# A hybrid attention and SSD layer in float32: attention in rounds of two units, first tables on another queue, softplus and one product moved

## The chip, the cores and the metric

One Trainium2 chip, one core. The metric is the device time of one execution in microseconds (us), as the median of several runs.

## What is computed

One decoder layer over 2048 positions of width 1024, batch 1, all in float32. A projection of the input gives q, k, v and a gate for 16 attention heads of 64, and the inputs of a Mamba-2 mixer with its gate and its step sizes. Attention is causal and runs three times, with dilations 1, 4 and 16, over a window of 128 steps; the three results are combined by a softmax over their log-sums. Both branches are gated and normed, projected together and normed with the residual.

```python
def dilated_window_attention(q, k, v, slopes, dilation):
    qb = to_blocks(q); kk = with_prev(to_blocks(k)); vv = with_prev(to_blocks(v))
    scores = jnp.einsum('bnqrhe,bnkrhe->bnrhqk', qb, kk)
    ...
    scores = jnp.where(valid, scores - slopes * dist, -jnp.inf)
    lse = jax.nn.logsumexp(scores, axis=-1)
    o = jnp.einsum('bnrhqk,bnkrhe->bnqrhe', jnp.exp(scores - lse[..., None]), vv)
...
wts = jax.nn.softmax(jnp.stack([l1, l2, l3], axis=0), axis=0)
y_att = wts[0] * o1 + wts[1] * o2 + wts[2] * o3
y_att = rms_norm(y_att * jax.nn.silu(z_att), att_norm_g)
dt = jax.nn.softplus(dt_raw + dt_bias)
y_ssm = rms_norm((ssd_chunked(xs, dt, -jnp.exp(a_log), b, c) + d_skip * xs) * jax.nn.silu(z_ssm), ssm_norm_g)
x = layer_norm(alpha * x + jnp.concatenate([y_att, y_ssm], -1) @ w_out, ln_g, ln_b)
```

## The kernel before

The program runs through three stages. In the **projections** (to 1197 us) the products of 2x2 blocks are formed by seven products of sums and differences; each operand is split into a high and a low part, and three matmuls (L340, L342, L344) make up one full product. `products` does seven such steps of twelve matmuls, with a `flush()` after each. `flush` counts and calls whatever was put down for that count in the table `later`: evacuations, weight loads, convolution taps, and the pieces of the generator `decays`. That generator computes the softplus of the step sizes on DVE (a polynomial: L496 and L497 once for each coefficient), then `adt`, a cumulative sum by matmul with a triangle (L510), and its transposes. Before, one piece is called at each count from 14 on, and every coefficient is a piece.

In **attention** (1198 to 1682 us) a unit is four blocks: two heads by two blocks of 128 queries. There are 8 pairs of heads, three dilations (d = 0, 1, 2), four groups `qd` and two halves: 192 units. A unit's scores (L894) go into two PSUM banks. DVE adds the table of biases and takes the minimum in one instruction (L900), ScalarE (ACT) takes the exponentials (L906), PE transposes them (L921), DVE copies the transposes to SBUF (L923), and PE multiplies by v (L947). A block whose keys reach into the block before has 192 columns of scores and not 128; the 64 remaining ones are transposed apart (L929) into a bank of the transposes, copied (L932) and multiplied by v too. That is so for all blocks but those at the start of a sequence, so d = 0 has none, and seven of the eight other groups of a pair have them. After both halves the accumulators N0 and N1, one bank each, are copied to SBUF by ACT (L971, L974, L977). `permute` on POOL reorders q and k for a dilation beforehand. The work of earlier pairs (softmax weights, combination, norm) is called at given units by the tables behind `todo`.

In the **output stage** (to the end) the SSM half is multiplied first, then the attention half (`product`, L1130 to L1132). POOL and DVE make high and low parts (L1098) and combine the last pair (L1038, L1042, L1053); the transposed statistics go through memory (L999, and back by a gather, L1005).

PE, DVE, ACT and POOL run their instructions in the order in which the code calls them; the order of the SyncE queue is set by the scheduler. The loop over the units, before:

```python
for i in range(len(todo) + TA + 1):
    if i < len(todo):
        pts[i] = scores(pairs[pr], d, qd, half)
    if 0 <= i - TA < len(todo):
        pts[i - TA] = transposes(d, qd, half, pts[i - TA])
    if i > TA:
        values(pairs[pr], d, qd, half, pts.pop(i - TA - 1))
```

Of the kernel before, what the change touches and what calls it, by code (L numbers as in the profile page):

```python
# [16 lines left out]
S = 2048  # L17
# [11 lines left out]
def hybrid_layer(ctx, tc, xT, xc, w52, wv, convw, convb, dtb, alog, dskp, gcol, wout,  # L29
# [53 lines left out]
    with ExitStack() as c1:  # L83
# [385 lines left out]
        def decays(dp):  # L469
# [249 lines left out]
        with tc.manual_schedule(engines={E.PE, E.DVE, E.Activation, E.Pool}):  # L719
# [9 lines left out]
            for j in range(16):  # L729
                later.setdefault(14 + j, []).append(lambda: next(dps, None))  # L730
# [66 lines left out]
    with ExitStack() as c2:  # L797
# [22 lines left out]
        def load_tab(A, d):  # L820
# [4 lines left out]
            nc.sync.dma_start(tb, tabs[2 * pr:2 * pr + 2, :, c0:c0 + tb.shape[2]].rearrange("h p c -> p h c"))  # L825
# [56 lines left out]
        def scores(A, d, qd, half):  # L882

            P = io.tile([128, 2, 512], F32, name="P", bufs=3)
            tab = A["tab"][d]
            sp = [psS.tile([128, 512], F32, name="S") for h in range(2)]
            for i in range(2):
                blk, cs = 4 * qd + 2 * i + half, cols(d, qd, half, i)
                for h in range(2):
                    for a in range(2):  # L890
                        o, kv = sp[h][64 * a:64 * a + 64, cs], keys(A, d, qd, 2 * i + half, h, a)
                        if d:
                            o = o.rearrange("p (c r j) -> p c r j", r=kv.shape[2], j=4)
                        nc.tensor.matmul(o, A["q"][d][64 * h:64 * h + 64, blk, 64 * a:64 * a + 64], kv,  # L894
                                         start=True, stop=True)
            for h in range(2):
                for i in range(2):
                    blk, cs = 4 * qd + 2 * i + half, cols(d, qd, half, i)
                    t = tab[:, h, 0:128] if cs.stop - cs.start == 128 else tab[:, h, 128:320]
                    nc.vector.tensor_tensor_reduce(P[:, h, cs], sp[h][:, cs], t, -0.125, 3.0e38, OP.add, OP.min,  # L900
                                                   accum_out=stat(A, 0, d, h, blk))
            for h in range(2):
                for i in range(2):
                    blk, cs = 4 * qd + 2 * i + half, cols(d, qd, half, i)
                    p = P[:, h, cs]
# [10 lines left out]

        def transposes(d, qd, half, P):
            tp = psT.tile([128, 2, 2, 128], F32, name="T")
            for h in range(2):
                for i in range(2):  # L920
                    nc.tensor.transpose(tp[:, h, i], P[:, h, 256 * i:256 * i + 128], ident)  # L921
            pt = io.tile([128, 2, 2, 128], F32, name="PT", bufs=4)
            nc.vector.tensor_copy(pt, tp)  # L923
            new = [i for i in range(2) if not first(d, qd, 2 * i + half)]
            if not new:
                return pt, None
            tc_ = psT.tile([128, 2, 2, 128], F32, name="T")
            for h in range(2):
                nc.tensor.transpose(tc_[:, 0, h], P[:, h, 128:256], ident)  # L929
            pc = io.tile([128, 2, 128], F32, name="PC", bufs=2)  # L930
            rows = slice(64 * new[0], 128)
            nc.vector.tensor_copy(pc[rows], tc_[rows, 0])  # L932
            return pt, pc

        def values(A, d, qd, half, pts):

            pt, pc = pts
            if half == 0:
                if qd == 0:
                    A["num"].append(cm_.tile([128, NR, NJ], F32, name="num", bufs=6))  # L940
# [3 lines left out]
            out = lambda i, h, lo, hi: A["N"][i][64 * h:64 * h + 64, 128 * half + lo:128 * half + hi]  # L944

            def mm(o, l, r, start):
                nc.tensor.matmul(o, l, r, start=start, stop=True, skip_group_check=True)  # L947
            for i in range(2):
                m = at(2 * i + half)
                if first(d, qd, 2 * i + half):  # L950
                    for h in range(2):
                        mm(out(i, h, 0, 128), v[:, m, 64 * h:64 * h + 64], pt[:, h, i], half == 0)
                    continue
                for a in range(2):
                    for h in range(2):
                        w = (v, vs)[a != i][:, m - (a == i == 0 or a != i), 64 * h:64 * h + 64]
                        mm(out(i, h, 64 * a, 64 * a + 64), w, pt[:, h, i, 64 * a:64 * a + 64], half == 0 and a == 0)
            for a in range(2):
                for i in range(2):
                    m, rows = at(2 * i + half), slice(64 * i, 64 * i + 64)  # L960
                    if first(d, qd, 2 * i + half):
                        continue
                    for h in range(2):
                        w = v[rows, m - i] if a == i else vs[rows, m - 2 * i]
                        mm(out(i, h, 64 * a, 64 * a + 64), w[:, 64 * h:64 * h + 64],
                           pc[rows, h, 64 * a:64 * a + 64], False)
            if half == 1:
                for i in range(2):
                    nm = A["N"][i][:, 0:256]
                    if d == 0:  # L970
                        nc.scalar.copy(f2(num[:, 4 * qd + 2 * i:4 * qd + 2 * i + 2, :]), nm)  # L971
                    elif d == 1:
                        o = num.rearrange("p (b s) (n a j) -> p n b a s j", b=4, a=2, j=16)[:, qd, 2 * i:2 * i + 2]
                        nc.scalar.copy(o, nm.rearrange("p (b a s j) -> p b a s j", b=2, a=2, s=4))  # L974
                    else:
                        j = 8 * (4 * qd + 2 * i)
                        nc.scalar.copy(num[:, :, j:j + 16].rearrange("p r (n j) -> p n r j", j=4),  # L977
                                       nm.rearrange("p (n r j) -> p n r j", r=16, j=4))
# [93 lines left out]

        def row():
            return f2(io.tile([128, 2, 512], F32, name="P", bufs=3))
# [43 lines left out]
        pns = ["N0", "N1"]  # L1118

        def product(n, br, hf):  # L1120
# [15 lines left out]
            pns.append(pns.pop(0))  # L1136
            pn = psN.tile([128, 512], F32, name=pns[0])
# [255 lines left out]
```

## Time and profile before

| what | before |
|---|---|
| median of 3 runs | 2076.76 us (2074.23 to 2078.97) |
| profiled execution | 2075.44 us |
| its span, first to last instruction | 2073.7 us |
| mean granted clock of TensorE | 0.980 |
| PE busy | 1979.9 us (95%) |
| DVE busy | 1234.0 us (60%) |
| ACT busy | 1121.9 us (54%) |
| POOL busy | 1077.9 us (52%) |

Busy time counts the instructions of an engine that does work, not its register and branch instructions. PE is TensorE's matmuls, PEld its loads of weights, which run beside them. The granted clock is a share of 2.4 GHz; the lower level is 1.2 GHz. A row in order of time gives start, duration, engine, line and operation, output and inputs, shapes, how many instructions of that kind follow each other; in brackets the idle time of the engine before it and what ended it. "issue" is time in which the engine waited for nothing that the profile shows.

### The profile page before, as it was taken

The numbers are of one execution on the slowest core, as the hardware profiler recorded it, in microseconds if no ns is written. First come the engines' busy times: TensorE is split into PE (matmuls) and PEld (weight loads), VectorE is DVE, ScalarE is ACT, GpSimd is POOL, SyncE is SP. The second block draws the span as 40 slices with busy tenths as digits, with TensorE's granted clock in tenths as the row PEclk, the third lists the DMA queues.
The fourth block names the chain that finished last, engine by engine and source line by source line (L and its number), as shares of the span: only waits on it lengthen the run. The fifth ranks groups of instructions, "written<-read, shape, count | busy, mean of one in ns | idle before, by whom it ended". The sixth has DMA issues, their size and how long they took to land.

```text
span 2073.7 us, 42402 instructions
## 1 busy us (share of the span) xinstructions
PE 1979.9 (95%) x15744; PEld 1616.6 (78%) x15744; DVE 1234.0 (60%) x3166; ACT 1121.9 (54%) x3095; POOL 1077.9 (52%) x963
## 2 busy tenths in 40 slices
PE   8999989889999999979999999999998979999998
PEld 8999778778887888858888867676766767888886
DVE  2353566357877656634444358777777846565553
ACT  3433445346655666536566478887887852232221
POOL 4545346556655666745555322787666572422222
PEclk9999999999999999989999999999999989999999
DMA  9897888967678877896877655788877799232220
GB/s 306 273 306 236 289 305 296 342 226 222 204 218 301 277 258 248 321 367 229 280 244 254 229 219 142 225 233 240 239 221 221 227 275 319 91 118 98 89 69 31
DMA packets 238846, 481.51 MB, mean 232 GB/s; under 512 B 38448, under 2 KB 111664, under 8 KB 226480
## 3 DMA queue, kind: packets, MB, share of 16 engines
q1 hardware_dynamic: 148464, 200.30, 30.8%
q0 software_dynamic: 44816, 180.71, 25.7%
q10 hardware_dynamic: 45360, 97.80, 14.5%
q8 instruction: 124, 2.03, 0.4%
q14 instruction: 82, 0.67, 0.1%
HBM read 323.15 MB, written 163.97 MB: 235 GB/s over the span
## 4 chain that ended last, share of the span: by engine, by line
PE 79%; DMA 7%; ACT 4%; DVE 4%; issue 3%; POOL 2%; SPq 1%; ACTq 0%; POOLq 0%; DVEq 0%
PE pp L340 12%; PE pp L342 11%; PE pp L344 11%; PE N L947 6%; PE pp L151 6%; PE S L894 4%; PE S L1130 4%; PE S L1132 4%; PE S L1131 4%; PE T L921 4%; PE ss L151 3%; ACT P L906 3%; PE T L1130 2%; PE T L1131 2%; PE T L1132 2%
## 5 line engine op out<-in xcount | busy, mean ns | idle before, releaser
L296 POOL TENSOR_TENSOR w<-wr,w 128x512 fp32r<-128x512 f32 x231 | 307.5, 1342 | 223.6 <-ACT w L295 174.5
L906 ACT ACTIVATE P<-P,st 128x192 f32<-128x192 f32 (+1 forms) x768 | 322.0, 421 | 77.3 <-DVE st L900 72.6
L900 DVE CUSTOM_DVE_ANT_0 P<-S,tb 128x192 f32<-128x192 f32 (+1 forms) x768 | 206.6, 324 | 101.3 <-PE S L894 75.7
L349 ACT COPY ev<-pp 128x512 f32<-128x512 f32 x176 | 103.1, 586 | 252.6 <-PE pp L344 227.5
L357 DVE TENSOR_TENSOR ev<-pp,ev 128x512 f32<-128x512 f32 x152 | 101.0, 685 | 149.7 <-PE pp L344 104.1
L295 ACT CAST w<-wr 128x512 fp32r<-128x512 f32 x231 | 139.7, 619 | 43.0 <-DVE wr L288 26.8
L1038 POOL TENSOR_TENSOR wb<-num,wb 128x2048 f32<-128x2048 f32 x21 | 95.7, 4556 | 117.6 <-DMA wb<-d_wd 63.9
L906 ACT ACTIVATION_READ_ACCUMULATOR P<-P,st 128x1 f32 x768 | 144.4, 188 | 0.0
L288 DVE TENSOR_TENSOR wr<-wr 128x512 f32<-128x512 f32 x132 | 123.3, 934 | 25.7 <-DMA wr<-w 21.1
L947 PE MATMUL N<-PT,v 128*64 128x64 f32 (+1 forms) x1536 | 127.1, 263 | 10.1 <-ACT num L971 7.7
L923 DVE COPY PT<-T 128x512 f32<-128x512 f32 x192 | 131.7, 686 | 6.1 <-PE T L921 6.1
L921 PE MATMUL T<-ident,P 128*128 128x128 f32 x768 | 128.8, 291 | 0.4 <-ACT num L977 0.2
L921 PEld LDWEIGHTS T<-ident,P 128*128 128x128 f32 x768 | 82.4, 143 | 48.4 <-issue 24.1
L894 PE MATMUL S<-k,ex 64*64 64x192 f32 (+1 forms) x2048 | 113.1, 332 | 4.7 <-issue 4.7
L947 PEld LDWEIGHTS N<-PT,v 128*64 128x64 f32 x1536 | 79.5, 139 | 48.0 <-issue 20.0
L441 DVE SCALAR_TENSOR_TENSOR ss<-U,cw,ss 128x512 f32<-128x512 f32 x144 | 105.9, 751 | 6.8 <-ACT ss L437 4.5
L122 POOL TENSOR_TENSOR vl<-vraw,vh 128x346 fp32r<-128x346 f32 (+1 forms) x48 | 48.5, 1011 | 91.6 <-ACT vh L121 88.3
L1168 POOL TENSOR_TENSOR k<-k,wb 128x1024 f32<-128x1024 f32 x8 | 25.8, 3227 | 121.9 <-DVE k L1167 121.9
L1106 DVE TENSOR_REDUCE tb<-P 128x128 f32<-128x1024 f32 x30 | 60.0, 2001 | 44.9 <-ACT P L1103 22.5
L894 PEld LDWEIGHTS S<-k,ex 64*64 64x64 f32 x2048 | 68.6, 138 | 17.4 <-issue 11.0
L564 ACT ACTIVATE mt<-csb,cs 128x128 f32<-128x128 f32 x256 | 78.5, 392 | 3.4 <-DMA csb<-d_cs 2.6
L573 DVE TENSOR_TENSOR mt<-mt,ss 128x1024 f32<-128x1024 f32 x32 | 39.0, 1220 | 65.8 <-ACT mt L569 65.4
(540 smaller groups left out, 6064.7 us busy)
## 6 DMA issues: line engine op xcount, KB each, us to landing
wr<-w ACTq DMA_DIRECT2D x157, 256.0 KB
wb<-d_wd SPq DMA_DIRECT2D x48, 512.0 KB
d_wc<-w SPq DMA_DIRECT2D x44, 512.0 KB
w<-d_wc POOLq DMA_DIRECT2D x44, 512.0 KB, 6.0
csb<-d_cs ACTq DMA_DIRECT2D x32, 512.0 KB
v<-d_v POOLq DMA_DIRECT2D x16, 1024.0 KB, 6.8
vs<-d_v POOLq DMA_DIRECT2D x16, 960.0 KB, 8.6
st<-xT POOLq DMA_DIRECT2D x20, 512.0 KB, 6.5
```

What stands on the lines that cost most here:

```text
L151: nc.tensor.matmul(ps, l if j == 2 else h, vw[k][j % 2], start=(k == j == 0), stop=(k == 7 and j == 2))
L295: nc.scalar.copy(t[:, 0], q[nm])
L296: nc.gpsimd.tensor_tensor(t[:, 1], q[nm], t[:, 0].bitcast(F32), op=OP.subtract)
L340: nc.tensor.matmul(ps, w[:, 0, k], th[:, k], start=start and k == 0, stop=False, skip_group_check=not start)
L342: nc.tensor.matmul(ps, w[:, 0, k], tl[:, k], start=False, stop=False, skip_group_check=not start)
L344: nc.tensor.matmul(ps, w[:, 1, k], th[:, k], start=False, stop=(k == 3), skip_group_check=not start)
L894: nc.tensor.matmul(o, A["q"][d][64 * h:64 * h + 64, blk, 64 * a:64 * a + 64], kv, start=True, stop=True)
L900: nc.vector.tensor_tensor_reduce(P[:, h, cs], sp[h][:, cs], t, -0.125, 3.0e38, OP.add, OP.min, accum_out=stat(A, 0, d, h, blk))
L906: nc.scalar.activation(p, p, AF.Exp, bias=stat(A, 0, d, h, blk), scale=-1.0, accum_out=stat(A, 1, d, h, blk))
L921: nc.tensor.transpose(tp[:, h, i], P[:, h, 256 * i:256 * i + 128], ident)
L923: nc.vector.tensor_copy(pt, tp)
L947: nc.tensor.matmul(o, l, r, start=start, stop=True, skip_group_check=True)
```

## The change

- `decays` stops only after the coefficients 11, 7 and 3, and its pieces are called at the counts 12, 13, 14, 19, 20, 21, 27 and 33.
- The first pair's three tables are loaded through POOL's queue, the first ahead of q and k.
- A round is two units. `scores` fills four banks for both halves; then come the values of the round before last, then the transposes of the last round. The eight exponentials of a round are split: five ahead of the accumulators' copies, three behind.
- The accumulators are one tile `N` of two banks, columns 0 to 255; the remainders' transposes go to columns 256 to 511 of the same banks and are copied by one instruction. At d = 0 both accumulators are copied by one instruction, alternately on DVE and on ACT.
- With the last pair, `split(0, 1)`, the low part of one half of the SSM branch on POOL, is called at (2, 0, 1) and (2, 1, 0) and not at (2, 1, 1) and (2, 2, 0).

```diff
@@ decays
             for m in (13, 11, 9, 7, 5, 3, 1):
                 nc.vector.tensor_tensor(h, h, z2, op=OP.mult)
                 nc.vector.tensor_scalar(h, h, 2.0 / m, None, op0=OP.add)
-                yield
+                if m in (11, 7, 3):
+                    yield
...
-            for j in range(16):
-                later.setdefault(14 + j, []).append(lambda: next(dps, None))
+            for j in (12, 13, 14, 19, 20, 21, 27, 33):
+                later.setdefault(j, []).append(lambda: next(dps, None))
@@ scores
-        def scores(A, d, qd, half):
+        def scores(A, d, qd):
...
-            sp = [psS.tile([128, 512], F32, name="S") for h in range(2)]
+            sp = [[psS.tile([128, 512], F32, name="S") for h in range(2)] for u in range(2)]
...
+            def exps(lo, hi):
+                for u, h, i, blk, cs in parts[lo:hi]:
...
-            return P
+            return P, exps
@@ transposes
-            tc_ = psT.tile([128, 2, 2, 128], F32, name="T")
-            for h in range(2):
-                nc.tensor.transpose(tc_[:, 0, h], P[:, h, 128:256], ident)
...
+            if new[0]:
+                tc_ = N[:, :, 256:512].rearrange("p u (h k) -> p u h k", h=2)
+                for u in range(2):
+                    for h in range(2):
+                        nc.tensor.transpose(tc_[:, u, h], P[:, u, h, 128:256], ident)
@@ values
-                A["N"] = [psN.tile([128, 512], F32, name=f"N{i}") for i in range(2)]
+        N = psN.tile([128, 2, 512], F32, name="N")
...
+            if d == 0:
+                evac(1 - qd % 2, num[:, 4 * qd:4 * qd + 4, :].rearrange("p (i b) j -> p i (b j)", i=2), N[:, :, 0:256])
+                return
@@ the loop
-            for i in range(len(todo) + TA + 1):
+            for n in range(len(todo) + 2):
...
+                        load_tab(pairs[0], 0, nc.gpsimd)
                         load_x(pairs[0], "q")
                         load_x(pairs[0], "k")
                         for k in range(3):
-                            load_tab(pairs[0], k)
+                            if k:
+                                load_tab(pairs[0], k, nc.gpsimd)
                             load_v(pairs[0], "v", k)
...
+                    made[n], exps = scores(pairs[pr], d, qd)
+                    exps(0, 5)
...
+                if n > 1:
+                    pr, d, qd = todo[n - 2]
+                    values(pairs[pr], d, qd, made.pop(n - 2))
+                if n < len(todo):
+                    exps(5, 8)
+                if 0 < n <= len(todo):
+                    made[n - 1] = transposes(*todo[n - 1][1:], made[n - 1])
...
+                    if pr == 7 and at in ((2, 0, 1), (2, 1, 0)):
+                        split(0, 1, slice(4 * qd, 4 * qd + 4), (0,))
+                    if pr == 7 and at == (2, 1, 0):
+                        split(0, 1, parts=(1,))
...
-                    if at in ((2, 1, 1), (2, 2, 0)):
-                        split(0, 1, slice(4 * qd - 4, 4 * qd), (0,))
-                    if at == (2, 2, 0):
-                        split(0, 1, parts=(1,))
```

VectorE (DVE) at the softplus, the difference of the two orders (h is the polynomial, z_2533 and z_2488 the same square under two numbers; L199, L202 and L357 belong to the projections):

```order
-L199 TENSOR_TENSOR st<-st 128x512
-L202 TENSOR_TENSOR to<-st,to 128x512
-L357 TENSOR_TENSOR ev<-pp,ev 128x512
-L496 TENSOR_TENSOR h<-h,z_2533 128x256
+L496 TENSOR_TENSOR h<-h,z_2488 128x256
 L497 TENSOR_SCALAR h<-h 128x256
```

The evacuations and sums that stood between two coefficients are no longer there; two coefficients follow each other.

PE in attention at d = 2, one unit before (S scores, T transposes, N accumulators, PT and PC the copied transposes and remainders):

```order
L894 MATMUL S<-k,ex 64x192 x8
L921 MATMUL T<-ident,P 128x128 x4
L929 MATMUL T<-ident,P 128x128 x2
L947 MATMUL N_13822<-PT,v 64x64 x2
L947 MATMUL N_13822<-PT,vs 64x64 x2
L947 MATMUL N_13823<-PT,vs 64x64 x2
L947 MATMUL N_13823<-PT,v 64x64 x2
L947 MATMUL N_13822<-PC,v 64x64 x2
```

and the end of a round in the changed kernel, with what it waits for:

```order
L965 MATMUL N<-PC,v 64x64 x2
L931 MATMUL T<-ident,P 128x128 [waits PE_49]
L931 MATMUL T<-ident,P 128x128 x3
L931 MATMUL T<-ident,P 128x128 [waits PE_49]
L931 MATMUL T<-ident,P 128x128 [waits Activation_49] x3
L939 MATMUL N<-ident,P 128x128 [waits Activation_49]
L939 MATMUL N<-ident,P 128x128 x3
L901 MATMUL S<-k,q 64x128 [waits DMASW0_49,DMASW1_49,DVE_49,PE_49]
```

The transposes come after the values of an older round and for two units at once; the remainders' (L939 after, L929 before) now write N and wait for ACT, and the next scores stand behind them.

POOL at the end of attention, before (wb is the last pair's combination, L1098 the low part, L1005 the gather of the statistics, the other DMAs weights and gates):

```order
L1038 TENSOR_TENSOR wb<-num,wb 128x2048
L1071 DMA v<-d_wo 128x2x512
L1240 DMA num<-d_za_83 128x2048
L1042 TENSOR_TENSOR wb<-wb 128x2048
L1071 DMA v<-d_wo 128x2x512
L1071 DMA vs<-d_wo 128x2x512
L1053 TENSOR_TENSOR wb<-wb 128x16x16x8
L1098 TENSOR_TENSOR num<-ex,num 128x1024
L1005 DMA cm<-d_st_132 128x6x32
```

and in the changed kernel (L1060, L1064, L1075, L1123 and L1027 are the same five):

```order
L1060 TENSOR_TENSOR wb<-num,wb 128x2048
L1093 DMA v<-d_wo 128x2x512
L1273 DMA num<-d_za_83 128x2048
L1123 TENSOR_TENSOR num<-ex,num 128x1024
L1064 TENSOR_TENSOR wb<-wb 128x2048
L1093 DMA v<-d_wo 128x2x512
L1093 DMA vs<-d_wo 128x2x512
L1075 TENSOR_TENSOR wb<-wb 128x16x16x8
L1027 DMA cm<-d_st_132 128x6x32
```

The low part stands ahead of the last two products of the combination; the gather is still behind them.

## Rows read from the trace of the kernel before

**Rows 1.** PE in order of time, around the softplus.
```profile
251.01 0.57 PE L340 MATMUL pp<-TT3h,w 128*128 128x512 f32 x1 [2.97 <-ACT ev L349]
...
272.28 1.19 PE L510 MATMUL ss<-adt,tri 128*128 128x256 f32 x2 [5.77 <-issue]
```
**Rows 2.** Windows: length, busy us of PE, PEld, DVE, ACT, POOL, clock, DMA share, GB/s.
```profile
250.00:255.00 5.00, 3.99 (x11) 3.13 (x12) 3.73 (x6) 2.10 (x4) 1.28 (x1) 0.66 0.51 174
270.00:275.00 5.00, 2.72 (x7) 2.21 (x8) 4.67 (x7) 2.01 (x3) 1.75 (x1) 0.68 0.78 315
```
**Rows 3.** DVE in order of time, around the softplus.
```profile
259.26 1.43 DVE L497 TENSOR_SCALAR h<-h 128x256 f32<-128x256 f32 x1
...
271.76 0.42 DVE L506 TENSOR_TENSOR adt<-dts,al 128x256 f32<-128x256 f32 x1
```
**Rows 4.** All engines in order of time, the start of attention.
```profile
1198.44 0.67 PE L894 MATMUL S<-k,q 64*64 64x128 f32 x16 [1.38 <-DVE ev L357]
...
1205.56 0.29 DVE L900 CUSTOM_DVE_ANT_0 P<-S,tb 128x128 f32<-128x128 f32 x1 [7.18 <-DMA tb<-tabs]
```
**Rows 5.** A window of 50 us in attention, columns as in rows 2.
```profile
1450.00:1500.00 50.00, 46.78 (x857) 34.66 (x857) 39.95 (x201) 41.41 (x185) 32.53 (x18) 0.97 0.80 233
```
**Rows 6.** PE in order of time, one unit at d = 2 and the next's scores.
```profile
1431.59 0.83 PE L894 MATMUL S<-k,ex 64*64 64x192 f32 x16
1432.35 0.66 PE L921 MATMUL T<-ident,P 128*128 128x128 f32 x4
...
1434.05 0.83 PE L894 MATMUL S<-k,ex 64*64 64x192 f32 x16
```
**Rows 7.** PE and DVE in order of time, three units at d = 0.
```profile
1386.96 0.67 PE L894 MATMUL S<-k,q 64*64 64x128 f32 x16
...
1388.41 0.29 DVE L900 CUSTOM_DVE_ANT_0 P<-S,tb 128x128 f32<-128x128 f32 x1
...
1388.62 0.69 DVE L923 COPY PT<-T 128x512 f32<-128x512 f32 x1
1388.73 0.67 PE L894 MATMUL S<-k,q 64*64 64x128 f32 x16
...
1390.70 0.67 PE L894 MATMUL S<-k,q 64*64 64x128 f32 x16
```
**Rows 8.** A window at d = 0, columns as in rows 2.
```profile
1386.96:1399.00 12.04, 11.80 (x187) 8.02 (x185) 10.39 (x59) 11.87 (x59) 8.07 (x15) 1.00 0.65 168
```
**Rows 9.** ACT in order of time, at d = 2.
```profile
1431.20 0.44 ACT L906 ACTIVATE P<-P,st 128x192 f32<-128x192 f32 x1
...
1432.19 0.65 ACT L977 COPY num<-N 128x256 f32<-128x256 f32 x2
```
**Rows 10.** PE's weight loads in order of time, at d = 2.
```profile
1432.35 0.42 PEld L921 LDWEIGHTS T<-ident,P 128*128 128x128 f32 x4 [0.28 <-ACT P L906]
...
1433.15 0.20 PEld L947 LDWEIGHTS N<-PT,v 128*64 128x64 f32 x4 [0.17 <-issue]
```
**Rows 11.** Waits of PE, 1195 to 1680: us in total, times, longest.
```profile
PE N L947 <- ACT num L971: 7.7, 7, 1.7
```
**Rows 12.** PE in order of time, after a wait at d = 2.
```profile
1302.11 0.27 PE L947 MATMUL N<-PC,v 64*64 64x64 f32 x2 [2.35 <-issue]
```
**Rows 13.** The window behind that wait, columns as in rows 2.
```profile
1302.11:1305.80 3.69, 3.69 (x51) 2.82 (x51) 1.95 (x10) 1.58 (x7) 3.69 (x1) 0.57 1.02 397
```
**Rows 14.** All engines in order of time, POOL's last products and the output product behind.
```profile
1679.76 4.54 POOL L1042 TENSOR_TENSOR wb<-wb 128x2048 f32<-128x2048 f32 x1
...
1690.18 2.33 POOL L1098 TENSOR_TENSOR num<-ex,num 128x1024 fp32r<-128x1024 f32 x1
...
1692.57 0.80 PE L1132 MATMUL S<-k,num 128*128 128x512 f32 x1 [9.32 <-POOL num L1098]
```
**Rows 15.** The window behind it, columns as in rows 2.
```profile
1692.57:1698.28 5.71, 5.71 (x14) 4.51 (x14) 3.52 (x3) 3.46 (x4) 1.36 (x2) 0.50 0.52 121
```
**Rows 16.** Waits of PE, 1680 to 2074: us in total, times, longest.
```profile
PE S L1130 <- DMA num<-d_wo: 3.0, 2, 1.6
```

More of the change, by code (lines that the diff above doesn't have):

```diff
@@ L915, in warm @@
                 nc.tensor.matmul(ps, x[:, 0, :], x[:, 4:8, :].rearrange("p r j -> p (r j)"), start=True, stop=True)
[L917 to L926, printed above, removed]
-            tc_ = psT.tile([128, 2, 2, 128], F32, name="T")
-            for h in range(2):
-                nc.tensor.transpose(tc_[:, 0, h], P[:, h, 128:256], ident)
[L930 to L940, printed above, removed]
-                A["N"] = [psN.tile([128, 512], F32, name=f"N{i}") for i in range(2)]
+        PC = io.tile([128, 2, 2, 128], F32, name="PC")
+        N = psN.tile([128, 2, 512], F32, name="N")
+        def transposes(d, qd, P):
+            pts = []
+            for u in range(2):
+                tp = psT.tile([128, 2, 2, 128], F32, name="T")
+                for h in range(2):
+                    for i in range(2):
+                        nc.tensor.transpose(tp[:, h, i], P[:, u, h, 256 * i:256 * i + 128], ident)
+                pts.append(tp)
+            new = [[i for i in range(2) if not first(d, qd, 2 * i + u)] for u in range(2)]
+            pc = None
+            if new[0]:
+                tc_ = N[:, :, 256:512].rearrange("p u (h k) -> p u h k", h=2)
+                for u in range(2):
+                    for h in range(2):
+                        nc.tensor.transpose(tc_[:, u, h], P[:, u, h, 128:256], ident)
+                pc = PC
+            for u in range(2):
+                pt = io.tile([128, 2, 2, 128], F32, name="PT", bufs=4)
+                nc.vector.tensor_copy(pt, pts[u])
+                pts[u] = pt
+            if new[0]:
+                if new[0] == new[1]:
+                    nc.vector.tensor_copy(pc, tc_)
+                else:
+                    for u in range(2):
+                        rows = slice(64 * new[u][0], 128)
+                        nc.vector.tensor_copy(pc[rows, u], tc_[rows, u])
+            return pts, pc
@@ L942, in values @@
+        def values(A, d, qd, made):
+            pts, pc = made
+            if qd == 0:
+                A["num"].append(cm_.tile([128, NR, NJ], F32, name="num", bufs=6))
             num, v, vs = A["num"][d], A["v"][d], A["vs"].get(d)
             at = lambda bq: 4 * bq + qd if d == 1 else 4 * qd + bq
-            out = lambda i, h, lo, hi: A["N"][i][64 * h:64 * h + 64, 128 * half + lo:128 * half + hi]
-            def mm(o, l, r, start):
-                nc.tensor.matmul(o, l, r, start=start, stop=True, skip_group_check=True)
@@ L948, in values @@
-            for i in range(2):
[L949 to L978, printed above, removed]
+            out = lambda b, h, lo, hi: N[64 * h:64 * h + 64, b // 2, 128 * (b % 2) + lo:128 * (b % 2) + hi]
@@ new lines, in values, with mm @@
+            begun = set()
+            def mm(b, h, lo, hi, l, r):
+                nc.tensor.matmul(out(b, h, lo, hi), l, r, start=(b // 2, h) not in begun, stop=True,
+                                 skip_group_check=True)
+                begun.add((b // 2, h))
+            for u in range(2):
+                for i in range(2):
+                    b, pt = 2 * i + u, pts[u]
+                    m = at(b)
+                    if first(d, qd, b):
+                        for h in range(2):
+                            mm(b, h, 0, 128, v[:, m, 64 * h:64 * h + 64], pt[:, h, i])
+                        continue
+                    for a in range(2):
+                        for h in range(2):
+                            w = (v, vs)[a != i][:, m - (a == i == 0 or a != i), 64 * h:64 * h + 64]
+                            mm(b, h, 64 * a, 64 * a + 64, w, pt[:, h, i, 64 * a:64 * a + 64])
@@ new lines, in values @@
+            for u in range(2):
+                for a in range(2):
+                    for i in range(2):
+                        b = 2 * i + u
+                        m, rows = at(b), slice(64 * i, 64 * i + 64)
+                        if first(d, qd, b):
+                            continue
+                        for h in range(2):
+                            w = v[rows, m - i] if a == i else vs[rows, m - 2 * i]
+                            mm(b, h, 64 * a, 64 * a + 64, w[:, 64 * h:64 * h + 64], pc[rows, u, h, 64 * a:64 * a + 64])
@@ L1071, in load_w @@
             nc.gpsimd.dma_start(W[e][:, :, s], d_wo[e][:, :, s])
+        at_row = [2, 0, 1]
         def row():
-            return f2(io.tile([128, 2, 512], F32, name="P", bufs=3))
+            at_row.append(at_row.pop(0))
+            return PB[:, D * at_row[0]:D * at_row[0] + D]
         def part(t, a):
```

86 lines of the change are left out of this document (43 added, 43 removed).

## The prediction

> **What bounds the kernel now.** I read the page's busy shares first and then each stage that the change touches, because a share of the whole span mixes stages with different limits. TensorE (PE) is busy for 95% of the span, so a part pays only where PE waits today, where its clock is low, or where PE itself gets less to do.
>
> In the projections the list of instructions in order of time shows PE two long waits around the softplus chain: 2.97 us, and 5.77 us ahead of the cumulative sum L510 [rows 1]. After both, the granted clock is low: 0.66 and 0.68 in the two windows [rows 2]. The reader is to see that the 5.77 us belong to work queued too early: L510 needs `adt`, which VectorE (DVE) writes at 271.76, half a microsecond before PE goes on [rows 3].
>
> At the start of attention the first scores are ready at 1199, but DVE takes them at 1205.56, after 7.18 us of waiting for a table [rows 4], which SyncE's queue loads.
>
> In steady attention (1450 to 1500) PE is busy 46.78 of 50 us, DVE 39.95 and ScalarE (ACT) 41.41, at a clock of 0.97 [rows 5]. Three engines are near their limit at once, so shorter PE work is worth only what the next one allows. A unit with remainders takes 2.46 us on PE, from scores at 1431.59 to scores at 1434.05, so two take 4.92 [rows 6]. With d = 0 two units take 3.74, from 1386.96 to 1390.70 [rows 7], while ACT is busy 11.87 of 12.04 us [rows 8]: this third is bound by ACT.
>
> **A, softplus.** Its arithmetic is the same; it is called in fewer, larger pieces, and the cumulative sum comes six flushes after `adt` instead of one. Removed: 2.97 + 5.77 = 8.7 us of waits [rows 1]. A window of 5 us at 0.66 to 0.68 of the full 2.4 GHz (a mix of that level and of 1.2 GHz) has lost 5 x 0.33 = 1.7 of PE's time [rows 2]; two of them are 3.4. Given back: the larger pieces put two polynomial terms in one flush. The second instruction of one term took 1.43 us in the worst case I found [rows 3]; one such on PE's path is about 1.5. Net 8.7 + 3.4 - 1.5 = 10.5 us. Low bound 5 (the 2.97 wait stays and so does its clock loss), high 12. What hides the polynomial itself is PE's twelve matmuls of a flush; if DVE is late there again, the wait would return at another flush.
>
> **B, first tables.** The first table goes through POOL's queue ahead of q and k, the other two between the loads of v; 7.18 us of DVE's wait end [rows 4] except for about 0.7, the scores' own length, 0.67 [rows 4], that DVE must wait for anyway: 6.5 us. What it is moved past there are the loads of q and k, each later by one table, and SyncE's queue has three loads less. If they are late next, the gain falls to 3, an estimate by half of the wait; with a clock loss like that of the softplus spared as well, it is 8.
>
> **C, rounds of two units.** The matrix work is equal: 32 score matmuls, 8 transposes, 4 for the remainders, 32 for the values. Three things change.
> First, at d = 0 one copy of 0.65 us [rows 9] alternates between DVE and ACT, so ACT loses half of 0.65, 0.33 a round. ACT is the bound there, and 3.74 becomes 3.41. DVE takes eight adds at a pitch of 0.21 and two copies of 0.69 [rows 7], 3.06, and with its half of the new copy 3.4: just as much. 8 pairs x 4 rounds x 0.33 = 10.6 us. The unit without copies took PE 1.77 us [rows 7], from 1386.96 to 1388.73; twice that, 3.54, leaves 0.20 a round: 6.4 is the low bound.
> Second, in each of 56 rounds with remainders (3 at d = 1, 4 at d = 2, 8 pairs) PE changes between tile shapes half as often. The weight loads show idle 0.28 us ahead of the transposes and 0.17 ahead of the values [rows 10], per unit. If all of that is on PE's path, a round saves 0.45; if PE's overlap hides most of it, 0.12. I take 0.25, near the middle, since a weight load that waits delays only a part of the matmuls behind it: 14 us, bounds 6.7 and 25.
> Third, a new wait. The remainders' transposes now write the two banks that the accumulators are copied out of, and so wait for ScalarE: five exps of the newer round at 0.44 (2.2) and copies of 0.65 [rows 9] stand ahead of them, and behind them on PE stand the next scores, which DVE and ACT wait for. Coming out of d = 0, where ACT lags, I expect PE to wait about 2.5 us at a pair's first round with remainders, where today seven waits for the copy add up to 7.7, or 1.1 each [rows 11]: 7 x 1.4 = 10 us. A wait of that length lowers the clock: after one of 2.35 us [rows 12] the next 3.69 us ran at 0.57 of full speed [rows 13], which loses 3.69 x 0.43 = 1.6. 7 x 1.6 = 11.
> Net 10.6 + 14 - 10 - 11 = 4 us, from -20 (the new wait in many rounds) to +27 (no new wait).
>
> Today the two copies of 0.65 us begin at 1432.19 and PE's transposes at 1432.35 [rows 6, 9], beside each other but in other banks. With accumulators and remainders in one bank the order makes PE wait for the whole copy. The Trainium skill ("PSUM — Partial Sum Buffer", PSUM bank collisions raise a hardware error) says that two engines must not touch one bank in the same partitions at once, whatever the columns, and to guard by bank; by that rule the 0.65 us stand in series with PE in every one of the 56 rounds, which speaks against this change and is the slower rival below; without it, only the first round of a pair would pay.
>
> **D, last pair.** The SSM half's low part on POOL (2.33 us at 1690.18) goes ahead of two products, of which the first starts at 1679.76 and takes 4.54 [rows 14]; it is ready 10.4 us earlier. PE waited 9.32 us for it, and ran at 0.50 for 5.71 us more [rows 15], which is 2.9 lost. Against it: the combination's products end 2.33 later, and with them the gather behind them and the last weights; PE today waits 3.0 us for the loads at that chain's end [rows 16], so a late chain shows there at once. The hooks of a unit also come after a round of two, some 3 us later. I take 7 of the 12 through, less 3: 4 us. Bounds 0 and 12.
>
> **Sum.** 10.5 + 6.5 + 4 + 4 = 25. The profiled execution took 2075.44 us (span 2073.7 and 1.7 around it), 1.3 under the median 2076.76 of the runs. 2075.44 - 25 = 2050.4, and with 1.3 the median is to be 2052.
>
> **Rivals.**
> 1. *No clock loss.* The wait at the first remainder round is short, or too short to lower the clock: 11 us come back: 2041. For: today's seven waits are 1.1 us. Against: five exps now stand ahead of the copies. Chance 0.22.
> 2. *Gains eaten.* DVE's larger softplus pieces stall PE elsewhere (A 5), q and k become late (B 4), C is nil, D 2: 11 us, 2066. For: DVE is busy 3.73 and 4.67 of 5 us beside the softplus [rows 2]. Chance 0.13.
> 3. *Slower: the copies set the round.* One loop runs through ACT, PE and DVE: five exps 2.2, copies 0.65 [rows 9], four transposes 0.66 [rows 6], the remainders' copy 0.69 and a first add 0.29 [rows 7], together 4.5 and the handoffs between them; PE's own round is 4.92 - 0.25 = 4.67. The first-round waits come out of d = 0 and stay. So at 4.67 + 25 / 56 = 5.12, five handoffs of 0.12, the whole gain is spent: that is the point from which this decides. At 5.4 the 56 rounds lose 41 us: 2093. For: ACT is busy 41.41 of 50 us already [rows 5]. Against: the exps start while the adds still run, so a late copy has some 0.2 us of room before PE sees it. Chance 0.10.
> 4. *Nothing moves.* The parts cancel: 2076. Chance 0.05.
>
> **How the numbers follow.** The forecast has 0.50 (own range 2044 to 2062), the rivals 0.22, 0.13, 0.10 and 0.05. A run of this kernel tells 0.2%, some 4 us, from no change. Faster: 0.50 + 0.22 + 0.13 = 0.85; same 0.05; slower 0.10. The range goes from 2035, rival 1 with D at 10 instead of 4, to 2072, rival 2 with B at its low bound, D at nothing and C at -3; left out are rivals 3 and 4 and the corners of 1: about 2 in 10.
>
> **What would show it.** Right: no wait ahead of the cumulative sum near 270 and a clock near 1 there; DVE's first add near 1199; a PE wait for the accumulator copy ahead of the remainders' transposes, about 2.5 us, once a pair, with a low clock behind it; two units at d = 0 in 3.4 us, with remainders in 4.7; the SSM product's wait for POOL a few us instead of 9.3, and more than 3.0 us of waits for the last loads. Wrong: remainder rounds of over 5 us (rival 3), no clock dips in attention (rival 1), or waits between the products while the softplus runs (rival 2).

## The result, and the profile after

| | before | after |
|---|---|---|
| median | 2078.44 us (6 runs) | 2086.99 us (6 runs) |
| span of the profile | 2073.7 us | 2084.4 us |
| first scores of attention | 1198.44 | 1197.82 |
| first output product | 1682.54 | 1695.50 |

The changed kernel is slower by 0.5% (ratio 1.005, interval 1.0034 to 1.0065). A gain of 25 us was forecast. The table's last rows place the loss: the projections end 0.6 us earlier, the output stage takes 2.3 us less, and attention 13.6 us more. Stage times are those of one execution of each kernel, and executions of one kernel differ by some us (the six of before by 6.8), so 2 us in a stage can be chance.

PE in order of time, around the softplus, after:

```profile
228.43 0.50 PE L340 MATMUL pp<-TT3h,w 128*128 128x512 f32 x1 [0.62 <-ACT ev L349]
...
241.03 0.50 PE L340 MATMUL pp<-TT2h,w 128*128 128x512 f32 x1 [1.43 <-ACT ev L349]
...
254.78 0.79 PE L340 MATMUL pp<-TT3h,w 128*128 128x512 f32 x1 [5.28 <-ACT ev L349]
```

DVE and ACT behind the last of these:

```profile
245.24 1.40 DVE L496 TENSOR_TENSOR h<-h,z 128x256 f32<-128x256 f32 x1
...
249.18 0.62 ACT L201 CAST to<-st 128x512 fp32r<-128x512 f32 x1 [5.11 <-DVE st L199]
...
253.62 0.62 ACT L201 CAST to<-st 128x512 fp32r<-128x512 f32 x1 [3.31 <-DVE st L199]
...
254.14 0.58 ACT L349 COPY ev<-pp 128x512 f32<-128x512 f32 x1
```

The wait ahead of the cumulative sum [rows 1] is gone, but the polynomial now fills DVE without a gap from 240.96 to 248.5. ACT stands at two casts (L201) for DVE's L199, 5.11 and 3.31 us, the evacuation L349 stands behind the second, and PE waits for the evacuation: 8.8 us in five waits where it was 8.7 in two. The clock loss has moved too (window columns as in rows 2):

```profile
255.00:260.00 5.00, 5.00 (x12) 3.90 (x13) 3.54 (x6) 1.73 (x4) 1.38 (x1) 0.50 0.92 252
```

DVE's own instructions are slow in this stretch where POOL works (DVE and POOL in order of time):

```profile
243.95 1.26 DVE L497 TENSOR_SCALAR h<-h 128x256 f32<-128x256 f32 x1
...
246.67 0.29 DVE L497 TENSOR_SCALAR h<-h 128x256 f32<-128x256 f32 x1
```

```profile
243.68 2.68 POOL L296 TENSOR_TENSOR w<-wr,w 128x512 fp32r<-128x512 f32 x2 [0.37 <-POOL w L296]
```

The same instruction takes 1.26 us beside POOL's L296 and 0.29 after it; the row of 1.43 us in [rows 3] also lies beside one. No run varies this alone.

The start of attention after, the scores of one round at d = 0 and of the next, and the first round with remainders of the second pair (PE and ACT in order of time):

```profile
1211.11 1.10 PE L901 MATMUL S<-k,q 64*64 64x128 f32 x32
...
1214.19 1.10 PE L901 MATMUL S<-k,ex 64*64 64x128 f32 x32
```

```profile
1276.41 0.46 ACT L911 ACTIVATE P<-P,st 128x192 f32<-128x192 f32 x1 [0.56 <-DVE st L905]
...
1278.17 0.44 ACT L911 ACTIVATE P<-P,st 128x192 f32<-128x192 f32 x1
...
1278.61 0.62 ACT L996 COPY num<-N 128x256 f32<-128x256 f32 x2
```

```profile
1279.28 0.66 PE L939 MATMUL N<-ident,P 128*128 128x128 f32 x4 [2.59 <-ACT num L996]
1279.87 2.00 PE L901 MATMUL S<-k,ex 64*64 64x192 f32 x32
```

A round at d = 0 takes 3.08 us instead of 3.74 [rows 7], more gain than forecast. The second and third fences show the new wait as drawn: five exponentials from 1276.41, the copies at 1278.61, and only then the remainders' transposes. One part was not drawn: ACT had stood 0.56 us for DVE's adds, which come behind the softmax weights of the pair before. In the first pair, which has no such weights, the wait is 1.80 us and not 2.59. Behind them the clock is low (window columns as in rows 2):

```profile
1279.28:1283.00 3.72, 3.72 (x58) 2.91 (x60) 3.15 (x17) 3.09 (x15) 0.00 (x0) 0.70 0.97 220
```

Waits of PE in attention, after (us in total, times, longest):

```profile
PE N L965 <- issue: 21.1, 10, 3.6
PE N L939 <- ACT num L996: 15.6, 8, 2.6
PE S L901 <- DVE st L905: 10.3, 5, 3.2
PE T L931 <- issue: 5.6, 2, 2.8
PE S L901 <- issue: 5.0, 4, 1.9
...
PE N L939 <- issue: 1.5, 1, 1.5
```

and the same view of before, of which [rows 11] has one line:

```profile
PE N L947 <- issue: 12.2, 6, 2.8
...
PE S L894 <- issue: 4.7, 2, 2.8
```

Two kinds of wait that the prediction left out have grown: "issue" from 16.9 to 33.2 us, and scores behind DVE's adds. The latter is a gather (DVE and PE in order of time):

```profile
1331.97 0.19 DVE L1034 TENSOR_TENSOR mm<-cm 128x32 f32<-128x32 f32 x1 [2.98 <-DMA cm<-d_st]
```

```profile
1333.38 2.90 PE L901 MATMUL S<-k,ex 64*64 64x192 f32 x32 [2.21 <-DVE st L905]
```

The weights' first instruction stands in DVE's order ahead of the adds, and the gather has not landed. The rounds between statistics and weights have become shorter, which I take for the reason.

**What "issue" is.** The DMA view, three adjoining stretches up to 1487 (queue, packets, MB, share of 16 engines), and the PE row behind them:

```profile
q1 hardware_dynamic: 213, 1.43, 100.9%
q14 instruction: 1, 0.01, 0.5%
...
q1 hardware_dynamic: 170, 0.28, 86.2%
q8 instruction: 1, 0.02, 5.7%
...
q0 software_dynamic: 182, 1.37, 89.9%
```

```profile
1484.58 0.27 PE L965 MATMUL N<-PT,v 128*64 128x64 f32 x2 [3.63 <-issue]
```

The queue q8 carries instructions, in 125 packets over the span, or 252 of PE's 31488 matmuls and weight loads for each. From 1474.8 to 1481.4 the engines are full of data and none of its packets comes; one lands between 1481.4 and 1482.9; PE, idle since 1480.95, goes on at 1484.58. In the DMA records a q8 packet stands so, ending some 1.2 to 1.8 us before PE goes on, at each of the eight issue waits of before and the sixteen of over half a microsecond of after. My reading: PE has used up its instructions, and the next ones queue behind data. Experiment 4 tests it.

**Where attention's time went**, from the starts of the 96 rounds in both traces: the first two rounds -6.1 us (the tables); all later ones +19.7. Of these: rounds 3 to 5 of each pair (d = 0) -15.8, round 6 -2.3; round 7, where the first remainders come, +20.4; rounds 8 to 12 +7.5; rounds 1 and 2 of the later pairs, where issue waits now fall, +9.9. The clock is part of this: in these later rounds it stood at 0.50 for 51.2 us where it had been 30.7, which costs PE about 10 us, an estimate by half of the difference.

### The profile page after: what moved, and what is told of

Its sections match the earlier page's. It is cut to its first block, busy times and chain, and to the rows that moved or that the text cites. A ratio compares the mean times of both kernels' runs of the same rounds, so it can differ in the third digit from the quotient of the medians.

```text
span 2084.4 us, 42689 instructions
## 1 busy us (share of the span) xinstructions
PE 1961.1 (94%) x15744; PEld 1635.2 (78%) x15744; DVE 1241.7 (60%) x3134; ACT 1109.5 (53%) x3049; POOL 1078.0 (52%) x966
## 4 chain that ended last, share of the span: by engine, by line
PE 74%; DMA 10%; DVE 6%; issue 5%; ACT 3%; POOL 2%; SPq 1%; ACTq 0%; POOLq 0%; DVEq 0%
PE pp L340 11%; PE pp L342 11%; PE pp L344 11%; PE pp L151 6%; PE N L965 4%; PE S L901 4%; PE S L1153 3%; PE ss L151 3%; PE S L1155 3%; PE S L1154 3%; PE T L931 3%; DVE P L905 2%; PE T L1153 2%; PE T L1154 2%; PE T L1155 2%
## 5 line engine op out<-in xcount | busy, mean ns | idle before, releaser
L296 POOL TENSOR_TENSOR w<-wr,w 128x512 fp32r<-128x512 f32 x231 | 306.5, 1338 | 223.4 <-ACT w L295 176.9
L349 ACT COPY ev<-pp 128x512 f32<-128x512 f32 x176 | 102.8, 584 | 244.5 <-PE pp L344 213.8
L905 DVE CUSTOM_DVE_ANT_0 P<-S,tb 128x192 f32<-128x192 f32 (+1 forms) x768 | 198.4, 324 | 15.5 <-PE S L901 14.6
L357 DVE TENSOR_TENSOR ev<-pp,ev 128x512 f32<-128x512 f32 x152 | 101.1, 686 | 135.1 <-PE pp L344 93.7
L943 DVE COPY PT<-T 128x512 f32<-128x512 f32 x192 | 123.9, 685 | 82.3 <-PE T L931 82.3
L1060 POOL TENSOR_TENSOR wb<-num,wb 128x2048 f32<-128x2048 f32 x21 | 95.5, 4546 | 121.0 <-DMA wb<-d_wd 101.5
L901 PE MATMUL S<-k,ex 64*64 64x192 f32 (+1 forms) x2048 | 108.6, 340 | 14.8 <-DVE st L905 10.3
L931 PE MATMUL T<-ident,P 128*128 128x128 f32 x768 | 109.7, 287 | 5.6 <-issue 5.6
L965 PE MATMUL N<-PT,v 128*64 128x64 f32 (+1 forms) x1536 | 106.3, 258 | 8.6 <-issue 6.5
L901 PEld LDWEIGHTS S<-k,ex 64*64 64x64 f32 x2048 | 76.3, 140 | 35.5 <-issue 24.5
L931 PEld LDWEIGHTS T<-ident,P 128*128 128x128 f32 x768 | 86.0, 145 | 17.4 <-issue 11.7
```

The lines of the kernel that those rows point to most:

```text
L296: nc.gpsimd.tensor_tensor(t[:, 1], q[nm], t[:, 0].bitcast(F32), op=OP.subtract)
L905: nc.vector.tensor_tensor_reduce(P[:, u, h, cs], sp[u][h][:, cs], t, -0.125, 3.0e38, OP.add, OP.min, accum_out=stat(A, 0, d, h, blk))
L931: nc.tensor.transpose(tp[:, h, i], P[:, u, h, 256 * i:256 * i + 128], ident)
L965: nc.tensor.matmul(out(b, h, lo, hi), l, r, start=(b // 2, h) not in begun, stop=True, skip_group_check=True)
```

## The experiments

**1. The parts alone.** `a_only` is the kernel before with the softplus hunks, `bd` with the tables and `split` hunks, `c_only` the changed kernel with those three undone.

> The kernel before with the softplus part of the change alone. Theory 4 (the waits only move: the larger pieces make DVE, then ACT's evacuation, late at another flush): 2078 within 3 us, with waits ahead of L340 of 8 us in total between 225 and 300. The prediction on record: 10.5 us less, 2068.

2073.95 us, ratio 1.0005 (0.9986 to 1.0024): no difference. Its trace has the moved waits around the softplus:

```profile
PE pp L340 <- ACT ev L349: 8.9, 4, 5.3
```

> The kernel before with the first tables through POOL's queue and the low part of the SSM half moved, nothing else. By the stages of the two traces (start of attention 6.1 us, output stage 2.0 us): 2076 - 8 = about 2068 (2065 to 2071). Rival (these gains need the other parts, or are noise between executions): 2074 to 2079.

2069.81 us, ratio 0.997 (0.9956 to 0.9984).

> The changed kernel with softplus, tables and low part as before: the rounds of two units alone. By the stages they cost 19.7 us, so 2076 + 20 = 2096 (2091 to 2100). Rival (the other parts cause some of the loss in attention, through times of loads or the place of the pieces): 2084 to 2089.

2095.61 us, ratio 1.009 (1.0073 to 1.0107). By the medians the three add up: 2 less (which is within the noise), 6.4 less and 19.4 more are 11 more, and 8.5 was measured. The rounds are the whole loss, and `bd`, the change without them, beats both kernels.

**2. Fewer exponentials ahead of the copies** (`exp2`).

```diff
-                    exps(0, 5)
+                    exps(0, 2)
...
-                    exps(5, 8)
+                    exps(2, 8)
```

> The changed kernel with two exponentials instead of five ahead of the accumulators' copies. Theory 1 (PE waits at a pair's first remainders because five exponentials and the copies stand ahead of them on ACT, and the clock falls behind that wait): three exponentials of 0.44 less in 8 places, so the 15.6 us of waits fall to about 5, and most of the low-clock stretches behind them (some 1.6 us each) go: 2087 - 10 - 10 = about 2067 (2061 to 2074). Rival 1 (the wait is for the copies or for the bank itself, whatever stands ahead): 2085 to 2089. Rival 2 (ACT then finishes the round's exponentials too late and the steady rounds of 4.78 us grow): 2090 and more.

2080.89 us, ratio 1.0025 (1.0009 to 1.0041): 6 us of the 20. Waits of PE in attention:

```profile
PE N L965 <- issue: 26.0, 12, 4.1
PE S L901 <- DVE st L905: 15.9, 6, 3.4
PE S L901 <- issue: 12.1, 6, 4.4
PE N L939 <- ACT num L996: 4.2, 6, 1.3
```

The mechanism of the wait holds (15.6 to 4.2), and some steady rounds fall to 4.63. But issue rises to 40.6 (with 2.5 at L931) and the wait on DVE by 5.6: what is saved is waited for elsewhere, and the time lies between theory 1 and rival 1. By the two traces attention is no shorter (498.6 us, 497.7 in the changed kernel); the gain is in the output stage (382.3 and 388.9), where the wait of 3.74 us for a weight load is 0.67.

**3. The weights one round later** (`wts`).

```diff
-                    if pr and at in ((0, 2, 1), (0, 3, 0)):
-                        weights(pairs[pr - 1], qd - 2)
+                    if pr and at in ((0, 3, 0), (1, 0, 0)):
+                        weights(pairs[pr - 1], d)
```

> The changed kernel with the two parts of the softmax weights of the last pair called one round later. Theory 2 (DVE stands at the weights' first instruction until the gather lands, because the rounds at d = 0 became shorter and only three of them lie between): the five waits of PE on DVE's adds, 10.3 us, go, one or two come back at the next wait: 2087 - 8 = about 2079 (2076 to 2082). Rival (the wait only moves, to the combination on POOL and the wait ahead of the remainders): 2085 to 2089.

2086.99 us: the rival. The wait on DVE is gone, the one for the copies has grown from 15.6 to 18.5, and one on POOL's reordering has come:

```profile
PE S L901 <- POOL ex L860: 11.9, 6, 4.1
```

**4. Fewer weight loads** (`light_after`, `light_before`).

```diff
-                wb = A["wb"] = cm_.tile([128, NR, NJ], F32, name="wb", bufs=3)
-                for h in range(2):
-                    nc.sync.dma_start(f2(wb[64 * h:64 * h + 64]),
-                                      dap(d_wd[pr], (d * 2 + h) * S, [[0, 64], [1, S]]))
-                eng.tensor_tensor(wb, A["num"][d], wb, op=OP.mult)
+                if k == 0:
+                    A["t"] = [cm_.tile([128, NR, NJ], F32, name="wb", bufs=3) for _ in range(3)]
+                    for h in range(2):
+                        nc.sync.dma_start(f2(A["t"][2][64 * h:64 * h + 64]),
+                                          dap(d_wd[pr], h * S, [[0, 64], [1, S]]))
+                wb = A["wb"] = A["t"][d]
+                eng.tensor_tensor(wb, A["num"][d], A["t"][2], op=OP.mult)
```

> The changed kernel, but the weights of dilation 1 are used for all three dilations, so that two thirds of the loads of the weights (2 of 3 MB a pair) are left out; POOL and all else do the same work. Theory 3 (PE's waits that the profile calls issue are waits for the next packet of its own instructions, which stands behind data on full DMA queues): these waits, some 33 us in attention, fall under 12 and the time falls by 20 to 30, to about 2062. Rival (they come from the order of the rounds or from semaphores): they stay, 2083 to 2089.

> The kernel before with the weights of dilation 1 for all three dilations, so that two thirds of the weight loads are left out, as in light_after. Theory 3 (packets of PE's own instructions wait behind data): its issue waits in attention, 16.9 us, fall under 4, and with the clock behind them the time falls by some 15 to 25, to about 2056; a smaller gain than in issue time for the changed kernel (33 us to 2), whose time fell by 16 because waits on POOL came in. Rival: no change, 2073 to 2079.

2070.77 us (ratio 0.997, 0.9957 to 0.9984) and 2068.11 (0.9955, 0.9941 to 0.997). The issue waits fall from 33.2 to 2.3 and from 16.9 to 0.2, so theory 3 holds for the waits. Its forecasts of the time, 2062 and 2056, failed: less is gained than the waits had cost, as other waits come in. The two kernels are now 2.7 us apart where it was 8.5, and their intervals overlap, so with the issue waits most of the difference goes. The waits in `light_after` and `light_before`:

```profile
PE S L901 <- POOL ex L860: 18.1, 12, 4.4
PE S L901 <- DVE st L905: 12.8, 6, 3.6
```

```profile
PE N L947 <- DVE PT L923: 18.3, 6, 4.2
```

**5. Smaller rows** (`exp2_wb2k`, from `exp2`).

```diff
-                for h in range(2):
-                    nc.sync.dma_start(f2(wb[64 * h:64 * h + 64]),
-                                      dap(d_wd[pr], (d * 2 + h) * S, [[0, 64], [1, S]]))
+                for c in range(4):
+                    for h in range(2):
+                        nc.sync.dma_start(f2(wb)[64 * h:64 * h + 64, 512 * c:512 * c + 512],
+                                          dap(d_wd[pr], (d * 2 + h) * S + 512 * c, [[0, 64], [1, 512]]))
```

> exp2 (two exponentials ahead of the copies) with each weight load issued as four loads of 512 columns, so in rows of 2 KB and not 8 KB. Theory 3b (an instruction packet waits behind single large rows in its DMA engine): the issue waits, 40.6 us in exp2, fall by half and the time from 2081 to about 2062. Rival (the queues' total load decides, or more small packets load them more): 2079 to 2090.

2091.93 us (ratio 1.0066, 1.0048 to 1.0085). Issue falls to 3.3 us, by more than theory 3b had it, yet the time rises, above the rival's range too: waits for k (21.2 us) and POOL (12.3) and one of 11.3 for a copy of the accumulators come in. The 24 issues take SyncE 17.75 us where six took 4.57, so the engines are less full from 1400 to 1415, in `exp2` and here:

```profile
1400.00:1415.00 15.00, 11.73 (x300) 9.90 (x292) 11.02 (x56) 10.24 (x46) 6.38 (x3) 1.00 0.95 206
```

```profile
1400.00:1415.00 15.00, 14.92 (x349) 12.57 (x343) 13.66 (x66) 13.45 (x61) 5.68 (x3) 1.00 0.56 173
```

With the DMA share at 0.56 instead of 0.95, PE is busy 14.92 of 15 us. The load has moved to the next 15 us, where the share is 0.97 and PE is busy 11.02 us (0.87 and 13.57 in `exp2`). Over 1197 to 1680 the share fell only from 0.72 to 0.67, so the mean load alone does not explain the issue waits. Whether the rows' size or the slower issue ended them stays open.

**6. POOL's additions left out too** (`thin_after`, `thin_before`, from the light kernels).

```diff
             elif k < 5:
-                eng.tensor_tensor(A["wb"], A["wb"], A["acc"], op=OP.add)
+                if last:
+                    eng.tensor_tensor(A["wb"], A["wb"], A["acc"], op=OP.add)
```

> light_after with the two additions of 4.5 us on POOL in each pair but the last left out as well. Theory 5 (without the issue waits a pair of heads is bound by a loop through POOL: gather, weights, products, reordering for the next pair, scores): its pairs of 60 to 61 us fall towards PE's own 51.6 us plus the wait at the first remainders, so some 5 us in each of 5 pairs or more: 2071 - 30 = about 2040 (2030 to 2052), with no wait on POOL left. Rival (PE, DVE and ACT bind the pair whatever POOL does): 2067 to 2073.

> light_before with the same additions left out. Theory 5: the pairs of 58 to 61 us fall to PE's own 55: 2068 - 15 to 22 = about 2050 (2044 to 2055); so the two kernels then stand about 10 us apart the other way round, and the rounds of two units show their worth. Rival: 2064 to 2070.

2031.72 (ratio 0.9796, 0.9768 to 0.9823) and 2032.27 us (0.98, 0.9772 to 0.9828). Theory 5 holds: 39 and 36 us less than the light kernels, for 9 us a pair on an engine that is busy half of the time. In `thin_before` the pairs of 58 to 61 us are 54.9, and PE hardly waits for POOL in either kernel. By the traces 37 and 25 us of it fall in attention; in `thin_before` another 12 fall in the output stage, where a wait of 12.2 us for POOL in `light_before` is gone. That POOL's additions had slowed DVE itself is not it: DVE's copies of the transposes take 0.69 us with and without them. `thin_before` went 12 us below its range, and the two kernels are level, not 10 us apart.

**7. The same with two exponentials** (`thin_exp2`: `thin_after` with the diff of experiment 2).

> thin_after (two thirds of the weight loads and two of POOL's additions left out) with two exponentials instead of five ahead of the copies. Theory 1 (the wait at the first remainders and the clock behind it are what the rounds of two units cost by themselves): the waits fall from 19.7 to about 5 us, steady rounds from 4.78 to 4.63, and now nothing takes it back: 2032 - 12 to 20 = about 2016 (2010 to 2022), clearly under thin_before's 2032. Rival (other waits take it back, as in exp2): 2027 to 2034.

2026.0 us (ratio 0.9754, 0.9729 to 0.9779), between the two theories. The wait halves (19.7 to 9.7), but the issue waits come back, 21 us in place of 6.7, even with a third of the weight loads:

```profile
PE N L965 <- issue: 12.3, 13, 3.4
PE N L939 <- ACT num L996: 9.7, 8, 1.3
PE S L901 <- issue: 6.3, 4, 2.6
PE T L931 <- issue: 2.5, 1, 2.5
```

**8. Attempts to loosen both bounds with the whole result.** `bd_spread` and `exp2_spread` issue the second and third weight load from POOL's queue, one step ahead of use; `bd_dve`, `after_dve` and `exp2_dve` put the two additions on DVE, in pieces of 512 columns, at (2, 2, 0), and the last product at (2, 2, 1). The cores of the two edits:

```diff
+                if k == 0 or last:
+                    fetch(d, nc.sync)
+                if k == 0 and not last:
+                    fetch(1, nc.gpsimd)
...
+                if k == 1 and not last:
+                    fetch(2, nc.gpsimd)
```

```diff
+                elif k == 4:
+                    a, b, c = [f2(t) for t in A["ws"]]
+                    for i in range(4):
+                        s = slice(512 * i, 512 * i + 512)
+                        nc.vector.tensor_tensor(b[:, s], b[:, s], a[:, s], op=OP.add)
+                        nc.vector.tensor_tensor(c[:, s], c[:, s], b[:, s], op=OP.add)
```

> bd with the weight loads of dilations 4 and 16 issued from POOL's queue one step ahead of the product that reads them, in place of all three at once from SyncE. Theory 3 (full DMA queues hold up PE's instruction packets): the issue waits in attention, 20 us in bd, fall by half or more and the time from 2070 to about 2060 (2054 to 2065). Rival (the loads now hold up POOL's loop or its loads of q and k): 2069 to 2078.

> exp2 with the same move of the weight loads. Theory 3: issue waits of 40.6 us fall by half and the time from 2081 to about 2066 (2058 to 2072). Rival (the loop through POOL takes the gain back, as in the run with rows of 2 KB): 2079 to 2090.

> bd with the two additions of each pair's combination but the last on DVE, in pieces of 512 columns at (2, 2, 0), and POOL's last product behind the reordering; all outputs computed. Theory 5 (a loop through POOL bounds a pair): POOL's loop is shorter by 9 us a pair, so the pairs of 58 to 59 us fall towards PE's 55, with the issue waits of about 20 us left: 2070 - 7 x 2 = about 2056 (2045 to 2064). Rival (the issue waits bound the pair, or DVE's additions delay its adds): 2068 to 2080.

> The changed kernel with the same additions on DVE. Theory 5: the five waits of PE behind DVE's gather (10.3 us) go, those at the first remainders and the issue waits stay: 2087 - 10 to 20 = about 2072 (2064 to 2080), so still some 15 us above bd_dve. Rival: 2084 to 2090.

> exp2 with the same additions on DVE. Theories 1 and 5 together: with the loop loosened the shorter wait at the first remainders (15.6 to 4 us) now counts, 10 us and the clock behind it: about 15 us under after_dve, 2057 (2048 to 2066), level with bd_dve. Rival (issue waits take it all): as after_dve, 2070 to 2080.

All are slower than forecast and than their starting points: 2106.84, 2093.56, 2117.87, 2112.79 and 2102.49 us, where the starting points took 2069.81, 2080.89, 2069.81, 2086.99 and 2080.89. In `bd_spread` issue falls only to 13.9 us and PE waits 26.6 us behind DVE's copies; each load is now a step of POOL's chain. In `bd_dve` the additions hold the tile that the gate is loaded into, and POOL stands up to 13.5 us in a pair:

```profile
1460.00 4.52 POOL L1062 TENSOR_TENSOR wb<-wb 128x2048 f32<-128x2048 f32 x1 [13.51 <-DMA wb<-d_za]
```

My expectations missed that both edits lengthen POOL's chain in time, though the second takes work from it. They do not measure what was asked; they show again that a later chain costs time.

## Why the prediction was wrong, point by point

The sum forecast was 10.5 + 6.5 + 4 + 4 = 25 us less. The traces show 0.6 + 6.1 - 19.7 + 2.3, so 10.7 us more, which is the difference of the two spans. A and C failed.

- **A, softplus: 10.5 forecast, 0.6 in the trace, nothing in `a_only`.** The step that failed is "one such on PE's path is about 1.5". I priced one slow instruction, not a queue: several pieces without a gap kept DVE for 7.5 us, and ACT, in order, passed the delay on to PE, 8.8 us of waits for the 8.7 removed. I also did not ask why that one instruction was slow (POOL beside it). Rival 2 had named the stall, but left half the gain standing.
- **B, tables: 6.5 forecast, 6.1 found.** Right: DVE's first add comes at 1198.52 and not at 1205.56.
- **C, d = 0: 10.6 forecast, 15.8 found** in rounds 3 to 5. I held ACT, and DVE with it, to be the limit at 3.41; PE does a round in 3.08 without a gap. Steady rounds with remainders fell short: from 4.93 to 4.78, 0.15 a round and not 0.25.
- **C, the new wait: 21 forecast** with its low clock, **about 15 found.** Right in place and cause, and `exp2` shows the cause. The waits are 15.6 us where they were 7.7, so 7.9 more for the 10 forecast. The clock fell behind three of them, some 7 us for the 11 forecast; behind the 2.59 us at 1531.73 it stayed at 1.00, so "a wait of that length lowers the clock" does not always hold. That the seventh round is 20.4 longer, so near 21, is luck: the waits of before fell in the sixth round, and some 6 us of the 20.4 are a low clock that begins behind the gather's waits of the sixth round (2.2 to 3.2 us in three pairs). The Trainium skill's rule ("PSUM — Partial Sum Buffer", PSUM bank collisions raise a hardware error) gives the order that makes PE wait; but only 13 of the 56 rounds show a wait for the copies, so it does not cost 0.65 us in each.
- **C, what was missing.** The step that failed is "Third, a new wait", as the only one. It put the issue waits at no change, though it priced the clock by one of them [rows 12]; they doubled, by 16 us. And the gather's wait was 10.3 where there was none (the 2.7 of before belong to the tables). With the clock behind them these turned C from +4 to -19.7, the far end of its bounds. I followed the delay as far as ACT. I should have asked when PE's instructions come, and how long the chain from gather to reordering takes, when rounds get shorter. Why there are twice as many issue waits is not shown: the number of packets is the same (124 and 125).
- **D: 4 forecast, 2.3 found.** The wait for POOL (9.32) is gone. Waits for weight loads of 3.7 and 1.0 us, and one of 3.8 us on DVE (L1169) at 1752.92, stand in its place:

```profile
1703.68 0.50 PE L1153 MATMUL S<-v,num 128*128 128x512 f32 x1 [3.74 <-DMA v<-d_wo]
```

- **Rival 3** had the sign but not the way: a steady round did not grow over 4.92; the loss is in single waits and the clock behind them. In no variant did the rounds of two units pay: without the issue waits and with POOL's chain short the changed kernel comes out level (experiment 6), and 6 us ahead with two exponentials (7, where the intervals still overlap), about what the tables and the low part give alone.

## What to carry to other kernels

An engine that is 95% busy with gaps of "issue" is not at its own limit: look at the DMA share and the instruction queue in just those gaps. Before counting a gain in each round, follow the longest chain that returns once per outer step (here gather, weights, products, reordering), through engines that look half idle. And a burst put on an in-order engine is to be priced by the whole queue behind it, not by its slowest instruction.

## What the hardware showed that I had not expected

PE's instructions come in packets, 125 over the span, that queue with the data: at a DMA share near 1 PE stood up to 3.6 us for one, and with two thirds of the weight loads left out 2.3 and 0.2 us in all of attention. After seven of the eight waits of before, and six of the sixteen of after, the granted clock is low too: 1480.95 to 1488.20, with its wait, shows 0.82. After the others, 2.81 us at 1292.19 among them, the next 3.7 us ran at 1.00.
